# Three plain tile pairs instead of two at the start of the MLP, with the Strassen input sums split one at a time between them

## The chip, the cores and the metric

The kernel runs on one core of a Trainium2 chip. The time is device microseconds (us) for one launch. The kernel before takes 1562.86 us, the median of three runs (1561.71 to 1564.18).

## The reference, cut to what matters

Two layers (`DEPTH = 2`) over 512 tokens of width 1024. In each layer an attention mixer and a convolution mixer are merged and added to the residual `x`; then comes the MLP, which is the part that the change touches:

```python
h = rmsnorm(x, g_ffn[i])
u = dwconv(h @ w_up[i], w_ffn_conv[i])        # w_up: 1024 x 5632, width-3 conv over tokens
a, val = u[..., :D_FF], u[..., D_FF:]         # D_FF = 2816
x = x + (jax.nn.silu(a) * val) @ w_down[i]
```

After it a gated per-layer embedding is added. Everything is float32.

## The kernel before, in words

**Precision.** Each float32 operand is split into two fp32r parts, high (`h`) and low (`l`): ScalarE casts the high part (L90, L103), VectorE subtracts it from the source to get the low part (L91, L104). A product then takes three matmuls, high by high, low by high and high by low (`mm3`, L97 to L100). `load` (L81) fetches a 128x1024 weight tile of 512 KB through the SP queue into one of three `raw` buffers; `wsplit` (L86) makes `wh`, `wl` from it, five buffers each.

**Where the MLP starts.** The output projection of the mixers (L546) ends with the norm of each of the four 128-token blocks (`after_o` calls `norm`, L124 to L139): square sum on ScalarE, reciprocal root on GpSimd, scaling on VectorE (L132), four transposes into PSUM (L135) and the split into `hh`, `hl`, the transposed normalised input. It also keeps an unsplit copy of it, in four quarters `hf` (L139): `h11`, `h12`, `h21`, `h22`, by token half and by input half.

**The up projection** has 22 pairs of 128-column output tiles (`NJ = 22`, one gate tile and one value tile to a pair). It is done in two ways.

- The first `NS = 2` pairs are plain: four tiles `eo` in four PSUM banks, each 8 k-tiles x 3 matmuls. They are done in two token halves, all four tiles on tokens 0 to 255 first and then on tokens 256 to 511 (L561 to L566), so that the first half can run while the last token blocks are still in their norm. That is 4 x 2 x 24 = 192 matmuls of 256 columns.
- The other 20 pairs use a Strassen-Winograd product of 2x2 blocks (`pair`, L597 to L647): seven products of 4 k-tiles x 3 matmuls x 256 columns, 84 matmuls to a pair, in place of eight. A generator yields between the products, so that two neighbouring pairs are interleaved. I call the products of pair j in their order y(j), x(j), z(j), and then four that accumulate into x and z.

A Strassen pair needs: two weight loads (`raw` and `rawp`, L598 and L600); the splits w0 (of `r0`) and w22 (`vh`, `vl`, two buffers each); four GpSimd differences of weight blocks in place (L605 to L608); then the splits w1 and w2 of the results (`th`, `tl`). On the input side it needs differences of the quarters: four VectorE operations on `hf` (L571 to L574), the splits of three of the results into `sums` (`sh`, `sl`, L576 to L578), and the split of `h21` back into a quarter of `hh`, `hl` (L579). VectorE also adds partial products in PSUM (L628, L641, L644).

**After a tile.** `taps` (L554) reads a finished PSUM bank: one ScalarE pass (L556) and two VectorE passes (L557, L558), the three taps of the convolution. The bank is free when the last of these has read it. `gated` (L589) does SiLU, product, and split into `gth`, `gtl`. PSUM has two banks `mm`, two `sc`, one `av` and three `tp`. The tiles take `mm` and `sc` in turn; in a Strassen pair y uses `av`, x is in an `mm` bank and z in an `sc` bank.

**What sets the order.** Outside the marked regions a list scheduler orders each engine's instructions: it simulates the kernel, and among the instructions that are ready in its simulation it takes the earliest written. Each engine then runs its list in that order. In a `manual_schedule` region (L684 to L706) the order of TensorE alone is that of the program text. Before the change the text has: the plain tiles' matmuls, the four sums, the three splits of sums and the split of h21, then `taps` and `gated` of the two plain pairs (L682, L683), then the region with the loop over Strassen pairs. From the fifth pair on `downs` interleaves pieces of the down projection (`ps_tp` matmuls of 512 columns) with the pairs.

Of the kernel before, what the change touches and what calls it, by code (L numbers as in the profile page):

```python
# [19 lines left out]
P = 128  # L20
# [4 lines left out]
KD = D // P  # L25
# [10 lines left out]
FF = 2816  # L36
NJ = FF // P
EPS = 1e-6
NS = 2
NQ = 5  # L40
HS = S // 2
MAGIC = 12582912.0
# [18 lines left out]
def encoder_kernel(ctx, tc, x_in, pT, pos, inv, w_a1, w_z, w_g, w_uq, w_ukv, w_au, w_cu, w_o,  # L61
# [11 lines left out]
    hh = cp.tile([P, NT, KD, P], F32R, name="hh")  # L73
    hl = cp.tile([P, NT, KD, P], F32R, name="hl")
# [3 lines left out]
    def psum(tag="mm"):  # L78
        return ps.tile([P, S], F32, tag=tag, name="ps_" + tag, bufs={"mm": 2, "av": 1, "sc": 2, "tp": 3}[tag])

    def load(src, n=1024):  # L81
        raw = wp.tile([P, n], F32, tag="raw", name="raw", bufs=3)
        nc.sync.dma_start(raw, src)
        return raw

    def wsplit(raw, n=1024, tag="w"):  # L86
        q, bufs = {"w": (wp, 5), "t": (ffp and ffp[-1], 4), "v": (ffp and ffp[-1], 2)}[tag]
        h = q.tile([P, n], F32R, tag=tag + "h", name=tag + "h", bufs=bufs)
        lo = q.tile([P, n], F32R, tag=tag + "l", name=tag + "l", bufs=bufs)
        nc.scalar.copy(h, raw)  # L90
        nc.vector.tensor_sub(lo, raw, h.bitcast(F32))  # L91
        return h, lo

    def weight(src, n=1024):
        return wsplit(load(src, n), n)

    def mm3(o, st, mv, start, stop, more=False):  # L97
        nc.tensor.matmul(o, st[0], mv[0], start=start, stop=False, skip_group_check=more)  # L98
        nc.tensor.matmul(o, st[0], mv[1], start=False, stop=False, skip_group_check=more)  # L99
        nc.tensor.matmul(o, st[1], mv[0], start=False, stop=stop, skip_group_check=more)  # L100

    def split(hi, lo, src):
        nc.scalar.copy(hi, src)  # L103
        nc.vector.tensor_sub(lo, src, hi.bitcast(F32))  # L104
# [95 lines left out]
    def layer(l, first):  # L200
# [64 lines left out]
        def t2(nm):  # L265
            return tmp.tile([P, S], F32, tag="t2", name=nm, bufs=4)

        def ws(o, w, rhs, nk, width, off, cols=slice(0, S), ks=None):
            for k in range(nk) if ks is None else ks:
                c = slice(k * width + off, k * width + off + P)  # L270
                mm3(o, (w[0][:, c], w[1][:, c]), (rhs[0](k, cols), rhs[1](k, cols)), k == 0, k == nk - 1)

        def hsel(b):
            return lambda k, c: b[:, c.start // P:c.stop // P, k, :]

        hT = (hsel(hh), hsel(hl))
# [277 lines left out]
        def taps(i, o):  # L554
            a = t2("fa")
            nc.scalar.activation(a, o, AF.Copy, scale=wfc[:, i, 1:2])  # L556
            nc.vector.scalar_tensor_tensor(a[:, 1:], o[:, :-1], wfc[:, i, 0:1], a[:, 1:], ALU.mult, ALU.add)  # L557
            nc.vector.scalar_tensor_tensor(a[:, :-1], o[:, 1:], wfc[:, i, 2:3], a[:, :-1], ALU.mult, ALU.add)  # L558
            return a

        ew = [weight(w_up[l, i]) for i in range(2 * NS)]  # L561
        eo = [psum("sc" if i % 2 else "mm") for i in range(2 * NS)]
        for half in range(2):
            c = slice(half * 256, half * 256 + 256)
            for i in range(2 * NS):
                ws(eo[i][:, c], ew[i], hT, KD, P, 0, c)  # L566
        quarter = [(slice(None), slice(2 * r, 2 * r + 2), slice(4 * k, 4 * k + 4), slice(None))
                   for r in range(2) for k in range(2)]
        V = nc.vector
        h11, h12, h21, h22 = hf  # L570
        V.tensor_tensor(h22, h22, h21, ALU.add)  # L571
# [1 line left out]
        V.tensor_tensor(h11, h22, h11, ALU.subtract)  # L573
        V.tensor_tensor(h12, h12, h11, ALU.subtract)  # L574
        sums = []
        for src in (h22, h11, h12):  # L576
            sums.append(tuple(ff.tile([P, 2, 4, P], F32R, tag="s", name=n, bufs=6) for n in ("sh", "sl")))
            split(*sums[-1], src)  # L578
        split(hh[quarter[2]], hl[quarter[2]], h21)  # L579

        def quart(r, k0):
            return lambda k: (hh[:, 2 * r:2 * r + 2, k0 + k, :], hl[:, 2 * r:2 * r + 2, k0 + k, :])

        def summed(i):
            return lambda k: (sums[i][0][:, :, k, :], sums[i][1][:, :, k, :])
# [3 lines left out]
        def gated(j, u):  # L589
            nc.scalar.activation(u[0], u[0], AF.Silu)  # L590
            nc.vector.tensor_tensor(u[1], u[0], u[1], ALU.mult)
            if j % 2 == 0:
                q, tag = (mid, "y") if j // 4 % 2 else (ff, "gt")
                gt[j // 2] = tuple(q.tile([P, 2, S], F32R, tag=tag, name=n, bufs=4) for n in ("gth", "gtl"))
            split(gt[j // 2][0][:, j % 2, :], gt[j // 2][1][:, j % 2, :], u[1])

        def pair(j):  # L597
            r0 = load(w_up[l, 2 * j])  # L598
            r1 = ff.tile([P, 1024], F32, tag="rawp", name="rawp", bufs=2)
            nc.sync.dma_start(r1, w_up[l, 2 * j + 1])  # L600
            b11, b21, b12, b22 = r0[:, :512], r0[:, 512:], r1[:, :512], r1[:, 512:]
            w0 = wsplit(r0)
            w22 = wsplit(b22, 512, "v")
            g = nc.gpsimd
            g.tensor_tensor(b22, b12, b22, ALU.subtract)  # L605
            g.tensor_tensor(b12, b12, b11, ALU.subtract)
            g.tensor_tensor(b11, b11, b22, ALU.subtract)
            g.tensor_tensor(b21, b21, b11, ALU.subtract)  # L608
            yield

            def product(o, w, off, mv, first):
                for k in range(4):
                    c = slice(off + k * P, off + k * P + P)
                    mm3(o, (w[0][:, c], w[1][:, c]), mv(k), first and k == 0, k == 3, not first)

            def side(nm):
                return ff.tile([P, HS], F32, tag="U", name=nm, bufs=4)

            y = psum("av")[:, :HS]
            product(y, w0, 512, quart(0, 4), True)  # L620
            w1 = wsplit(r1, 1024, "t")
            yield
            m0 = psum("mm")
            x = m0[:, HS:]
            product(x, w0, 0, quart(0, 0), True)
            Y = side("Y")
            nc.scalar.copy(Y, y)
            V.tensor_tensor(m0[:, :HS], x, Y, ALU.add)  # L628
            w2 = wsplit(r0, 1024, "t")
            yield  # L630
            m1 = psum("sc")
            z = m1[:, :HS]
            product(z, w1, 0, summed(0), True)
            yield
            product(x, w2, 0, summed(1), False)
            U, Z = side("U"), side("Z")
            nc.scalar.copy(U, x)  # L637
            nc.scalar.copy(Z, z)
            yield
            product(x, w1, 512, quart(1, 0), False)  # L640
            V.tensor_tensor(m1[:, HS:], x, Z, ALU.add)  # L641
            yield
            product(z, w22, 0, summed(2), False)
            V.tensor_tensor(z, z, U, ALU.add)  # L644
            yield
            product(x, w2, 512, quart(1, 4), False)
            gated(j, [taps(2 * j, m0), taps(2 * j + 1, m1)])  # L647
# [30 lines left out]
        def advance(g, n=1):  # L678
            for _ in range(n if g else 0):
                next(g, None)  # L680

        for j in range(NS):  # L682
            gated(j, [taps(2 * j + i, eo[2 * j + i]) for i in range(2)])  # L683
        region = tc.manual_schedule(engines={mybir.EngineType.PE})  # L684
        region.__enter__()
        old, new = None, pair(NS)
        advance(new)
        for q in range(NS, NJ + 1):
            nxt = pair(q + 1) if q + 1 < NJ else None
            advance(old)  # L690
# [11 lines left out]
            old, new = new, nxt  # L702
# [45 lines left out]
    for l in range(L):  # L748
        layer(l, l == 0)
# [79 lines left out]
```

## Time and profile before

| | |
|---|---|
| median of 3 runs | 1562.86 us (1561.71 to 1564.18) |
| profiled execution | 1562.61 us, span of its trace 1560.7 us |
| mean granted TensorE clock | 0.991 |
| TensorE busy | 1515.9 us, 97% of the span |
| VectorE busy | 1039.4 us, 67% |
| ScalarE busy | 792.5 us, 51% |
| GpSimd busy | 326.2 us, 21% |

The sum of the prediction is made against the profiled execution: 1562.61 us, of which 1.9 us lie outside the span of the trace; it is 0.25 us below the median. A row of the timeline has start and duration in us, the engine, the line, the operation with output and inputs, and in brackets the idle time before it and what released it. Matmuls overlap: a 256-column matmul lasts 0.28 us by its row, but the next one starts 0.12 us after it, so prices are taken from start to start. PEld is the weight load that goes with each matmul. A row of a windows table has the stretch, its length, each engine's busy time with its count of instructions, then the granted clock, the share of the DMA engines and GB/s. A row of the waits has the total, the number of times and the longest. The MLP of layer 0 starts at 359 us of the trace and that of layer 1 at 1131 us.

### The profile page before, as it was taken

How to read it: one execution, taken by the hardware profiler on the slowest of the kernel's cores; microseconds unless marked ns; L12 is line 12 of the kernel's file. 1: busy time of each engine (PE TensorE's matmuls, PEld its weight loads, DVE VectorE, ACT ScalarE, POOL GpSimd, SP SyncE). 2: the span in 40 equal slices, each digit the busy share in tenths (PEclk: the TensorE clock that was granted, in tenths of full speed). 3: DMA queues.
4: the chain of work that ended last, by engine and by line, in shares of the span. 5: the costliest groups of instructions: out<-in, count | busy, mean ns of one | idle time of the engine just before them, and what ended most of it. 6: DMA issues, size and time to landing. Idle time of an engine off the chain costs nothing.

```text
span 1560.7 us, 22378 instructions
## 1 busy us (share of the span) xinstructions
PE 1515.9 (97%) x8776; PEld 1326.0 (85%) x8776; DVE 1039.4 (67%) x1492; ACT 792.5 (51%) x1312; POOL 326.2 (21%) x313
## 2 busy tenths in 40 slices
PE   7999999998799999999999999999979999999998
PEld 6888888888789999998888888888878999999886
DVE  7778553438787777767477776343497877777763
ACT  6678632326455455534374887232364545454452
POOL 2800000004233232310045000000043333333000
PEclk9999999999899999999999999999989999999999
DMA  6211123322333323233142102233133332333321
GB/s 208 89 58 41 55 95 94 95 82 80 98 109 95 111 93 109 96 108 108 58 135 81 41 28 82 81 107 96 55 104 101 103 114 94 105 98 97 109 75 61
DMA packets 41448, 142.32 MB, mean 91 GB/s; under 512 B 5760, under 2 KB 6272, under 8 KB 41344
## 3 DMA queue, kind: packets, MB, share of 16 engines
q1 hardware_dynamic: 41344, 140.90, 28.4%
q8 instruction: 69, 1.13, 0.3%
q14 instruction: 35, 0.29, 0.1%
HBM read 138.78 MB, written 2.10 MB: 90 GB/s over the span
## 4 chain that ended last, share of the span: by engine, by line
PE 87%; DVE 6%; DMA 2%; ACT 2%; POOL 2%; issue 1%; SPq 0%; DVEq 0%; ACTq 0%
PE ps_mm L99 13%; PE ps_mm L98 13%; PE ps_mm L100 13%; PE ps_sc L100 8%; PE ps_sc L98 7%; PE ps_sc L99 7%; PE ps_tp L99 5%; PE ps_tp L100 5%; PE ps_tp L98 5%; PE ps_av L98 2%; PE ps_av L99 2%; PE ps_av L100 2%; PE ps_tp L438 2%; DVE wl L91 1%; DVE tl L91 1%
## 5 line engine op out<-in xcount | busy, mean ns | idle before, releaser
L90 ACT CAST wh<-raw 128x1024 fp32r<-128x1024 f32 (+1 forms) x210 | 218.1, 1044 | 304.1 <-PE ps_mm L99 91.2
L91 DVE TENSOR_TENSOR wl<-raw,wh 128x1024 fp32r<-128x1024 f32 (+1 forms) x210 | 260.9, 1251 | 152.4 <-ACT wh L90 150.9
L98 PE MATMUL ps_mm<-hh,wh 128*128 128x512 f32 (+1 forms) x672 | 245.9, 366 | 12.0 <-DVE fa L558 11.4
L99 PE MATMUL ps_mm<-hl,wh 128*128 128x512 f32 (+1 forms) x672 | 241.8, 360 | 0.0
L100 PE MATMUL ps_mm<-hh,wl 128*128 128x512 f32 (+1 forms) x672 | 241.6, 360 | 0.0
L108 POOL TENSOR_SCALAR ms<-ms 128x1 f32<-128x1 f32 (+2 forms) x40 | 13.2, 329 | 759.3 <-ACT junk L127 728.5
L98 PEld LDWEIGHTS ps_mm<-hh,wh 128*128 128x128 f32 x672 | 127.6, 190 | 30.3 <-issue 11.7
L100 PEld LDWEIGHTS ps_mm<-hh,wl 128*128 128x128 f32 x672 | 127.6, 190 | 20.0
L99 PEld LDWEIGHTS ps_mm<-hl,wh 128*128 128x128 f32 x672 | 127.9, 190 | 17.4
L605 POOL TENSOR_TENSOR rawp<-rawp 128x512 f32<-128x512 f32 x40 | 55.5, 1388 | 388.5 <-DVE vl L91 388.5
L99 PE MATMUL ps_tp<-wl,gth 128*128 128x512 f32 x320 | 126.4, 395 | 0.0
L98 PE MATMUL ps_tp<-wh,gth 128*128 128x512 f32 x320 | 126.4, 395 | 0.0
L100 PE MATMUL ps_tp<-wh,gtl 128*128 128x512 f32 x320 | 126.4, 395 | 0.0
L556 ACT ACTIVATE fa<-ps_mm,wfc 128x512 f32<-128x512 f32 x44 | 30.4, 690 | 134.8 <-PE ps_mm L100 134.7
L98 PE MATMUL ps_mm<-hh,th 128*128 128x256 f32 x320 | 89.4, 280 | 2.6 <-ACT U L637 2.6
L535 DVE TENSOR_TENSOR xs<-xs,ps_tp 128x512 f32<-128x512 f32 x80 | 54.7, 684 | 53.2 <-PE ps_tp L100 52.9
L99 PE MATMUL ps_mm<-hl,th 128*128 128x256 f32 x320 | 89.1, 278 | 0.0
L100 PE MATMUL ps_mm<-hh,tl 128*128 128x256 f32 x320 | 89.0, 278 | 0.0
L100 PEld LDWEIGHTS ps_tp<-wh,gtl 128*128 128x128 f32 x320 | 60.1, 188 | 14.5
L98 PEld LDWEIGHTS ps_tp<-wh,gth 128*128 128x128 f32 x320 | 60.2, 188 | 11.4
L99 PEld LDWEIGHTS ps_tp<-wl,gth 128*128 128x128 f32 x320 | 60.1, 188 | 11.2
L557 DVE SCALAR_TENSOR_TENSOR fa<-ps_mm,wfc,fa 128x511 f32<-128x511 f32 x44 | 32.9, 748 | 49.7 <-ACT fa L556 49.7
(297 smaller groups left out, 4198.5 us busy)
## 6 DMA issues: line engine op xcount, KB each, us to landing
raw<-in_w_up_dram SPq DMA_DIRECT2D x48, 512.0 KB, 3.8
raw<-in_w_down_dram SPq DMA_DIRECT2D x44, 512.0 KB, 3.7
rawp<-in_w_up_dram SPq DMA_DIRECT2D x40, 512.0 KB, 3.6
raw<-in_w_g_dram SPq DMA_DIRECT2D x32, 512.0 KB, 3.6
raw<-in_w_z_dram SPq DMA_DIRECT2D x24, 512.0 KB, 3.7
raw<-in_w_o_dram SPq DMA_DIRECT2D x16, 512.0 KB, 3.5
raw<-in_w_pg_dram SPq DMA_DIRECT2D x16, 512.0 KB, 3.7
raw<-in_w_au_dram SPq DMA_DIRECT2D x8, 512.0 KB, 3.7
```

Of the source, the lines that this page charges most:

```text
L90: nc.scalar.copy(h, raw)
L91: nc.vector.tensor_sub(lo, raw, h.bitcast(F32))
L98: nc.tensor.matmul(o, st[0], mv[0], start=start, stop=False, skip_group_check=more)
L99: nc.tensor.matmul(o, st[0], mv[1], start=False, stop=False, skip_group_check=more)
L100: nc.tensor.matmul(o, st[1], mv[0], start=False, stop=stop, skip_group_check=more)
L108: nc.gpsimd.tensor_scalar_add(ms, ms, EPS)
L438: nc.tensor.transpose(tp[:, k * P:(k + 1) * P], pe[:, k * P:(k + 1) * P], ident)
L535: nc.vector.tensor_tensor(xs[:, t, c], xs[:, t, c], o, ALU.add)
L556: nc.scalar.activation(a, o, AF.Copy, scale=wfc[:, i, 1:2])
L557: nc.vector.scalar_tensor_tensor(a[:, 1:], o[:, :-1], wfc[:, i, 0:1], a[:, 1:], ALU.mult, ALU.add)
L605: g.tensor_tensor(b22, b12, b22, ALU.subtract)
```

## The change

`NS` becomes 3 and a new constant `NE` is 3. The first three plain tiles (`NE`) are done in token halves as before. The TensorE region begins before the taps. In it a loop over the three plain pairs makes the remaining tiles 3, 4 and 5, each in one piece of 512 tokens, does `taps` and `gated` of the pair, and then splits one of the three sums. After the second plain pair (`j == 1`), pair 3, now the first Strassen pair, is created and its first step is written: its two loads, w0, w22 and its four GpSimd differences. The split of `h21` comes after the loop. The four additions of L571 to L574 stay where they are, ahead of the loop. Strassen pairs are 3 to 21, 19 to a layer in place of 20; the main loop starts at q = 3.

```diff
-NS = 2
+NS = 3
+NE = 3
...
-        ew = [weight(w_up[l, i]) for i in range(2 * NS)]
-        eo = [psum("sc" if i % 2 else "mm") for i in range(2 * NS)]
+        ew = [weight(w_up[l, i]) for i in range(NE)]
+        eo = [psum("sc" if i % 2 else "mm") for i in range(NE)]
         for half in range(2):
             c = slice(half * 256, half * 256 + 256)
-            for i in range(2 * NS):
+            for i in range(NE):
                 ws(eo[i][:, c], ew[i], hT, KD, P, 0, c)
-        quarter = [(slice(None), slice(2 * r, 2 * r + 2), slice(4 * k, 4 * k + 4), slice(None))
-                   for r in range(2) for k in range(2)]
...
         sums = []
-        for src in (h22, h11, h12):
+
+        def sumsplit(src):
             sums.append(tuple(ff.tile([P, 2, 4, P], F32R, tag="s", name=n, bufs=6) for n in ("sh", "sl")))
             split(*sums[-1], src)
-        split(hh[quarter[2]], hl[quarter[2]], h21)
...
-        for j in range(NS):
-            gated(j, [taps(2 * j + i, eo[2 * j + i]) for i in range(2)])
         region = tc.manual_schedule(engines={mybir.EngineType.PE})
         region.__enter__()
-        old, new = None, pair(NS)
-        advance(new)
+        for j in range(NS):
+            u = []
+            for i in (2 * j, 2 * j + 1):
+                if i >= NE:
+                    eo.append(psum("sc" if i % 2 else "mm"))
+                    ws(eo[i], weight(w_up[l, i]), hT, KD, P, 0)
+                u.append(taps(i, eo[i]))
+            gated(j, u)
+            sumsplit((h22, h11, h12)[j])
+            if j == 1:
+                old, new = None, pair(NS)
+                advance(new)
+        q = (slice(None), slice(2, 4), slice(0, 4), slice(None))
+        split(hh[q], hl[q], h21)
         for q in range(NS, NJ + 1):
```

## Prediction

> **What bounds the kernel now.** I read the page first, then TensorE's waits, then the timeline of the MLP's start engine by engine, then windows.
>
> ```profile
> span 1560.7 us, 22378 instructions
> PE 1515.9 (97%) x8776; PEld 1326.0 (85%) x8776; DVE 1039.4 (67%) x1492; ACT 792.5 (51%) x1312; POOL 326.2 (21%) x313
> ```
>
> TensorE is the bound over the whole span; a change can win only what TensorE waits for, or what it does slowly. Who makes it wait:
>
> ```profile
> PE ps_mm L98 <- DVE fa L558: 11.4, 2, 5.7
> PE ps_sc L98 <- DVE fa L558: 7.2, 2, 3.6
> PE ps_sc L100 <- DVE tl L91: 5.9, 4, 1.9
> PE ps_mm L98 <- ACT U L637: 2.6, 3, 1.6
> ```
>
> The two largest are each met twice, once a layer: a Strassen product waits for the last tap (L558) of a plain tile, which holds its PSUM bank. All four lie at the start of the MLP. TensorE's timeline there, layer 0:
>
> ```profile
> 358.97 0.29 PE L98 MATMUL ps_mm<-hh,wh 128*128 128x256 f32 x1
> ...
> 367.81 0.60 PE L135 MATMUL ps_tp<-ident,ht 128*128 128x128 f32 x4
> ...
> 383.27 0.28 PE L98 MATMUL ps_av<-hh,wh 128*128 128x256 f32 x1
> ...
> 384.56 0.28 PE L100 MATMUL ps_av<-hh,wl 128*128 128x256 f32 x1
> 390.52 0.55 PE L98 MATMUL ps_mm<-hh,wh 128*128 128x256 f32 x1 [5.68 <-DVE fa L558]
> ...
> 393.00 0.41 PE L100 MATMUL ps_mm<-hh,wl 128*128 128x256 f32 x1
> 397.04 0.55 PE L98 MATMUL ps_sc<-sh,th 128*128 128x256 f32 x1 [3.62 <-DVE fa L558]
> ...
> 404.43 0.39 PE L98 MATMUL ps_mm<-hh,th 128*128 128x256 f32 x1 [1.62 <-ACT U L637]
> ...
> 418.26 0.39 PE L98 MATMUL ps_sc<-sh,th 128*128 128x256 f32 x1 [0.74 <-ACT th L90]
> ...
> 420.70 0.58 PE L100 MATMUL ps_sc<-sh,tl 128*128 128x256 f32 x1 [1.93 <-DVE tl L91]
> ...
> 433.68 0.39 PE L100 MATMUL ps_sc<-sh,tl 128*128 128x256 f32 x1 [1.41 <-DVE tl L91]
> ```
>
> The plain tiles run from 358.97 without a wait. The first product of pair 2 follows at 383.27; then x(2) waits, z(2) waits, and smaller waits follow to 433.68. The clock falls too:
>
> ```profile
> 390.00:391.00 1.00, 0.48 (x2) 0.51 (x3) 1.00 (x3) 0.55 (x1) 0.84 (x1) 0.50 0.47 188
> ...
> 421.00:422.00 1.00, 1.00 (x6) 1.00 (x6) 1.00 (x3) 0.62 (x1) 0.00 (x0) 0.50 0.49 66
> ```
>
> After each long stall the granted clock is 0.50 for a while: the 11 steps from 390.52 to 393.00 take 2.48 us, and the same 11 from 383.27 to 384.56 take 1.29. A dozen matmuls at the low clock cost 1.2 us extra.
>
> The cause is VectorE's list:
>
> ```profile
> 370.41 1.23 DVE L571 TENSOR_TENSOR hf<-hf 128x1024 f32<-128x1024 f32 x1 [0.65 <-ACT hf L139]
> ...
> 378.51 2.32 DVE L574 TENSOR_TENSOR hf<-hf 128x1024 f32<-128x1024 f32 x1
> ...
> 382.99 0.74 DVE L557 SCALAR_TENSOR_TENSOR fa<-ps_mm,wfc,fa 128x511 f32<-128x511 f32 x1
> ...
> 389.64 0.74 DVE L558 SCALAR_TENSOR_TENSOR fa<-ps_mm,wfc,fa 128x511 f32<-128x511 f32 x1
> ...
> 402.58 0.68 DVE L104 TENSOR_TENSOR gtl<-fa,gth 128x512 fp32r<-128x512 f32 x1
> ```
>
> None of the later rows has an idle time in brackets: VectorE is full from 370.4 to 403, and tile 0's second tap is run only at 389.64, behind sums and weight splits. So the stage has both a full engine and a bad order on it. The size of the loss:
>
> ```profile
> 1131.13:1155.43 24.30, 24.30 (x209) 24.29 (x208) 20.71 (x20) 15.86 (x23) 10.27 (x7) 1.00 0.32 112
> 1155.43:1206.26 50.83, 38.03 (x279) 36.75 (x278) 44.24 (x52) 26.39 (x39) 19.47 (x12) 0.87 0.30 93
> 358.97:383.27 24.30, 24.30 (x210) 24.30 (x208) 20.71 (x20) 15.86 (x23) 10.27 (x7) 1.00 0.37 112
> 383.27:436.42 53.15, 38.15 (x278) 36.89 (x277) 44.22 (x52) 26.27 (x39) 19.49 (x12) 0.87 0.29 88
> ```
>
> The windows end where the first matmul of a down piece starts. The second window of each layer holds 23 products of 12 matmuls, 276. At full speed:
>
> ```profile
> 369.19 0.28 PE L98 MATMUL ps_sc<-hh,wh 128*128 128x256 f32 x1
> ...
> 371.89 0.28 PE L100 MATMUL ps_sc<-hh,wl 128*128 128x256 f32 x1
> ...
> 436.42 0.39 PE L98 MATMUL ps_tp<-wh,gth 128*128 128x512 f32 x1
> ...
> 438.99 0.39 PE L100 MATMUL ps_tp<-wh,gtl 128*128 128x512 f32 x1
> ```
>
> 23 steps of a 256-column matmul take 2.70 us, 0.1175 each; 11 of a 512-column one take 2.57, 0.2335 each. 276 x 0.1175 = 32.4 us. The loss is 53.15 - 32.4 = 20.7 us in layer 0 and 50.83 - 32.4 = 18.4 in layer 1, **39.1 us in all**. That is the most that can be won.
>
> **The change part by part.**
>
> *More matmul work.* Before: 192 x 0.1175 = 22.56 plus a Strassen pair of 84 x 0.1175 = 9.87, 32.43 us a layer. After: three tiles in halves, 144 x 0.1175 = 16.92, and three whole, 72 x 0.2335 = 16.81, 33.73. **+1.3 us a layer, +2.6**. It is on the path, with certainty.
>
> *Shorter cover for the last norm.* Token block 3's transposes end at about 368.4 (row at 367.81), and its splits just after:
>
> ```profile
> 368.39 1.37 DVE L104 TENSOR_TENSOR hl<-ps_tp,hh 128x512 fp32r<-128x512 f32 x2 [2.42 <-ACT hh L103]
> ```
>
> The first half of three tiles is 72 x 0.1175 = 8.5 us plus the 16 transposes (24.30 - 22.56 = 1.7 us), so TensorE would want block 3 at 358.97 + 10.2 = 369.2; the first of the two splits ends near 369.1, the second at 369.76 and is wanted four k-tiles (1.4 us) later. Before, one more tile (2.8 us) covered this. I take 0.5 us a layer, between 0 and 2.8.
>
> *The two big waits.* The halves end at 358.97 + 16.92 + 1.7 = 377.6; tile 3 runs to 383.2, tile 4 to 388.8, tile 5 to 394.4; then y(3), x(3), z(3) at 394.4, 395.8, 397.2. Tile 4 reuses the bank of tile 0 and tile 5 that of tile 1; x(3) needs taps of tile 2, z(3) those of tile 3. The taps of tiles 0 and 1 are now written ahead of all splits of sums and of all weight splits but the first tiles'. VectorE has, from 370.4: four sums at 1.23 (4.9 us), then taps of two tiles at 2 x 0.74 each (3.0). They end near 379 by the price of the rows, and tile 4 wants the first at 383.2. So both waits, 5.68 and 3.62, and the 2.4 us of low clock behind them go, unless the order says otherwise (a rival).
>
> *What is late next.* VectorE's work up to z(4), at 394.4 + 7 x 1.41 = 404.3: four sums 4.9; twelve tap passes 8.9; nine subtractions of 1024 columns (wl of tiles 4, 5 and of w0 of two pairs; tl of both first parts and the first pair's second; two sums) and h21's,
>
> ```profile
> L91 DVE TENSOR_TENSOR wl<-raw,wh 128x1024 fp32r<-128x1024 f32 x31 | 37.2, 1222 | 10.6 <-ACT wh L90 10.6
> ```
>
> 10 x 1.22 = 12.2; eight passes of 512 or 256 columns at no more than 0.68 (two vl, two products, two gtl, two adds), some 5.0. That is 31 us in 33.9 (370.4 to 404.3). To it comes GpSimd's toll:
>
> ```profile
> 379.71 2.28 POOL L605 TENSOR_TENSOR rawp<-rawp 128x512 f32<-128x512 f32 x1
> ...
> L91 DVE TENSOR_TENSOR wl<-raw,wh 128x1024 fp32r<-128x1024 f32 x3 | 5.8, 1935 | 0.0
> ```
>
> L574 takes 2.32 us in GpSimd's company where L571 took 1.23, and three wl between 370.4 and 403 took 1.94 each against 1.22 later: 1.1 + 3 x 0.72 = 3.3 us, and I take 4 for two pairs. So 35 in 33.9: VectorE is about just in time, and z(4) waits by 0 to 5 us. I take 2.4, and 1.0 more for a dozen matmuls at the low clock behind it.
>
> The Trainium skill ("SBUF — State Buffer", section "Who interferes with whom") says that a VectorE instruction with two SBUF inputs and a GpSimd one that reads SBUF exclude each other, the later waiting for the whole of the other. By this rule the change doesn't remove the toll, it moves it under the plain tiles; the 2.32 us agrees.
>
> *The vh chain.* vh, vl have two buffers, so a pair's w22 waits for the product of two pairs earlier:
>
> ```profile
> 410.95 0.61 ACT L90 CAST vh<-rawp 128x512 fp32r<-128x512 f32 x1
> ...
> 413.31 1.30 POOL L605 TENSOR_TENSOR rawp<-rawp 128x512 f32<-128x512 f32 x1 [22.47 <-DVE vl L91]
> ...
> 418.69 1.96 DVE L91 TENSOR_TENSOR tl<-rawp,th 128x1024 fp32r<-128x1024 f32 x1
> ```
>
> From vh to the end of tl lie 9.7 us, with five products (7.1 us) between in TensorE's order. Before, pairs 4 and 5 pay it with no down piece as cover (0.74 + 1.93, and 1.41). After, pair 4 is only the second Strassen pair and finds a free buffer; pair 5 still pays: 1.6 a layer, between 0.7 and 2.7. The wait for U (1.62 in layer 0, 2.6 in both) comes from ScalarE's queue behind a down weight that is still loading; nothing in the change removes it; 1.0 a layer.
>
> *Queues passed.* Pair 3's two loads go ahead of tiles 4 and 5 in SP's text and its GpSimd work ahead of their matmuls.
>
> ```profile
> raw<-in_w_up_dram SPq DMA_DIRECT2D x48, 512.0 KB, 3.8
> ```
>
> At 3.8 us a load, with three buffers that come free as the first tiles' splits end (before 370), tiles 4 and 5 have their weights ahead of 383 and 389; what hides this is tile 3's 5.6 us. Behind a late load would wait ScalarE's casts, then taps. I put it at nothing, up to 2 us.
>
> **The sum.** What stays a layer: 0.5 + 2.4 + 1.0 + 1.6 + 1.0 = 6.5 us. 1562.61 - 39.1 + 2.6 + 2 x 6.5 = **1539 us**. The median stands 0.25 above the profiled run, which is nothing here. The terms' ends, 2 to 11 a layer, give 1530 to 1548.
>
> A clock rule: the trace grants 0.50 at 421 after 0.74 and 1.93 us of idle with two matmuls between. The Trainium skill ("TensorE: Matmul & The Clock Gate", "HAM oscillation — how this bites in real kernels") asks for an idle gap of some 3.4 us before the clock drops. By the page the 1.0 us of low clock would be 0 and the sum 1537; the row speaks for keeping it.
>
> **The rivals.**
> 1. *VectorE's backlog only shifts* (0.15). Its work up to the fourth pair grows by two splits, two tiles' taps and a gate, 2.4 + 3.0 + 1.4 = 6.8 us, TensorE's cover by tiles 4 and 5, 11.2; if throughput and not order made the 12 us of the two waits and their clock, 12 - (11.2 - 6.8) = 7.6 stay beside the 4 to 6 elsewhere, 13 a layer: 1562.6 - 39.1 + 2.6 + 26 = 1552. For it: no idle VectorE for 33 us. Against: much of what ran there wasn't due yet.
> 2. *Tile 4 takes over the wait: slower* (0.08). If the scheduler leaves tile 0's second tap where it is (end 390.4), tile 4, due at 383.2, waits 7.2 us in place of x(2)'s 5.8, and all else behind it stays: 1.4 + 1.3 a layer, 1568. It decides for any tap end after about 388. Against: the splits that stood ahead of it are now written after it.
> 3. *Nearly all of it goes* (0.14): the later waits were echoes of the first stall. 1 to 2 us stay a layer: 1562.6 - 39.1 + 2.6 + 3 = 1529.
> 4. *It doesn't matter* (0.03): the waits reappear behind tile 5 in equal size, within 3 us of 1562.
>
> **How the numbers follow.** The forecast has 0.60. A measurement can tell about 0.2%, 3 us, from no change. Faster: 0.60 + 0.15 + 0.14 = 0.89; same 0.03; slower 0.08. The range goes from rival 3's end to just past rival 1: 1528 to 1555.
>
> **What would show it.** In the profile after: waits for L558 near zero; TensorE unbroken from 359 to about 397, with 72 matmuls of 512 columns more a layer (whole plain tiles); clock 1.00 there; tile 0's second tap before 383; one wait at a Strassen z for tl of 1 to 3 us in place of two; U's still there. A gap ahead of the 512-column plain tiles would be rival 2, gaps of 5 us after 395 rival 1, and a gap near 369 would mean that three tiles don't cover the norm.

## The result and the profile after

The changed kernel takes **1547.28 us** (median of four runs, 1546.78 to 1548.68). The kernel before, run beside it, takes 1562.78 (1561.71 to 1564.18). The ratio is 0.9902 with a 95% interval of [0.9885, 0.9919]: faster by 15.5 us, about two thirds of the 23.5 that were forecast. The time lies in the predicted range, 8 us above the predicted value. The profiled execution of after is the slowest of its four, 1548.68 us.

The page, its span and its first engine row:

```profile
span 1546.9 us, 22111 instructions
PE 1514.3 (98%) x8656; PEld 1318.1 (85%) x8656; DVE 1029.3 (67%) x1482; ACT 788.4 (51%) x1302; POOL 309.3 (20%) x305
```

TensorE's busy time hardly moves (1515.9 before) while the span falls by 13.8 us. So most of the gain is waiting that went away. What is left of the four waits that the prediction showed:

```profile
PE ps_mm L99 <- DVE fa L559: 14.5, 2, 7.2
...
PE ps_sc L101 <- DVE tl L92: 1.1, 2, 0.6
```

The columns are the total, the number of times and the longest. Line numbers up to the taps are one higher than before: L559 is the last tap, which was L558. The two large waits of before (5.7 and 3.6 a layer) have become one of 7.2 a layer, the waits at `tl` fell from four to two, and the wait for U is gone. TensorE's timeline at the start of layer 0's MLP, from the end of tile 3:

```profile
383.24 0.39 PE L101 MATMUL ps_sc<-hh,wl 128*128 128x512 f32 x1
390.87 0.76 PE L99 MATMUL ps_mm<-hh,wh 128*128 128x512 f32 x1 [7.24 <-DVE fa L559]
...
396.55 0.41 PE L100 MATMUL ps_mm<-hl,wh 128*128 128x512 f32 x1
...
404.75 0.28 PE L99 MATMUL ps_av<-hh,wh 128*128 128x256 f32 x1
...
425.78 0.39 PE L101 MATMUL ps_sc<-sh,tl 128*128 128x256 f32 x1 [0.56 <-DVE tl L92]
...
428.51 0.39 PE L99 MATMUL ps_tp<-wh,gth 128*128 128x512 f32 x1
```

The halves and tile 3 run without a gap; the last matmul of tile 3 starts at 383.24, within 0.3 us of what was worked out. Then tile 4 (390.87) waits for tile 0's second tap, whose bank it takes: this is the gap that the prediction named as the sign of its second rival. Behind it 13 matmuls run at the low clock, 5.68 us (390.87 to 396.55) where 13 x 0.2335 = 3.04 were due. From there to the first down piece at 428.51 only 0.56 us is waited for; y(3), x(3) and z(3) (404.75 to 407.56) follow tile 5 without a gap.

The loss of the stage, reckoned as in the prediction: from the end of tile 3 (383.24 + 0.23) to the first down piece, in each layer.

```profile
383.47:428.51 45.04, 37.24 (x241) 33.94 (x241) 39.36 (x47) 24.88 (x35) 11.20 (x8) 0.89 0.30 96
1147.50:1192.75 45.25, 37.44 (x243) 34.11 (x241) 39.61 (x47) 25.06 (x35) 11.32 (x8) 0.89 0.30 96
```

It holds tiles 4 and 5, 48 matmuls at 0.2335, and 16 products, 192 at 0.1175: 33.8 us at full speed. The loss is 11.3 us in layer 0 and 11.5 in layer 1, where before it was 20.7 and 18.4. Put into the prediction's sum: 1562.6 - 39.1 + 2.6 + 22.8 = 1548.9, and the profiled run shows 1548.7. So nothing outside these windows moved and the added matmul work was right; the residual was taken at 13 and is 22.8.

VectorE's list up to the tap that tile 4 waits for, every row:

```profile
370.54 1.23 DVE L571 TENSOR_TENSOR hf<-hf 128x1024 f32<-128x1024 f32 x1 [0.65 <-ACT hf L140]
371.80 1.22 DVE L572 TENSOR_TENSOR hf<-hf 128x1024 f32<-128x1024 f32 x1
372.94 0.69 DVE L92 TENSOR_TENSOR vl<-rawp,vh 128x512 fp32r<-128x512 f32 x1
373.54 1.22 DVE L573 TENSOR_TENSOR hf<-hf 128x1024 f32<-128x1024 f32 x1
374.68 2.32 DVE L105 TENSOR_TENSOR sl<-hf,sh 128x1024 fp32r<-128x1024 f32 x1
376.92 1.79 DVE L92 TENSOR_TENSOR vl<-rawp,vh 128x512 fp32r<-128x512 f32 x1
378.63 2.32 DVE L92 TENSOR_TENSOR wl<-raw,wh 128x1024 fp32r<-128x1024 f32 x1
380.87 2.31 DVE L574 TENSOR_TENSOR hf<-hf 128x1024 f32<-128x1024 f32 x1
383.11 0.74 DVE L558 SCALAR_TENSOR_TENSOR fa<-ps_mm,wfc,fa 128x511 f32<-128x511 f32 x1
383.77 1.64 DVE L92 TENSOR_TENSOR wl<-raw,wh 128x1024 fp32r<-128x1024 f32 x1
385.33 2.28 DVE L105 TENSOR_TENSOR sl<-hf,sh 128x1024 fp32r<-128x1024 f32 x1
387.53 0.74 DVE L558 SCALAR_TENSOR_TENSOR fa<-ps_sc,wfc,fa 128x511 f32<-128x511 f32 x1
388.19 1.21 DVE L92 TENSOR_TENSOR tl<-rawp,th 128x1024 fp32r<-128x1024 f32 x1
389.32 0.73 DVE L558 SCALAR_TENSOR_TENSOR fa<-ps_mm,wfc,fa 128x511 f32<-128x511 f32 x1
389.99 0.73 DVE L559 SCALAR_TENSOR_TENSOR fa<-ps_mm,wfc,fa 128x511 f32<-128x511 f32 x1
```

Tile 0's second tap runs at 389.99. Before the change it ran at 389.64, though it is now written ahead of two splits of sums and of other pairs' weight splits. Seven rows that the prediction left behind the taps stand ahead of this one: two `vl`, two `sl`, two `wl` and a `tl`. From start to start they take, in the order of this sentence, 0.60 + 1.71 + 2.24 + 2.20 + 2.24 + 1.56 + 1.13 = 11.7 us: about what lies between the 379 at which the prediction let the taps end and the 390.7 of the trace. Six of the rows are longer than the same operations elsewhere (four of 2.3 and one of 1.64 against 1.22, one of 1.79 against 0.69). GpSimd runs beside them, and is itself slowed, from 1.30 for one alone to between 1.63 and 2.28:

```profile
376.00 2.16 POOL L606 TENSOR_TENSOR rawp<-rawp,raw 128x512 f32<-128x512 f32 x1
378.24 1.63 POOL L607 TENSOR_TENSOR raw<-raw,rawp 128x512 f32<-128x512 f32 x1
379.83 2.28 POOL L605 TENSOR_TENSOR rawp<-rawp 128x512 f32<-128x512 f32 x1
```

### The profile page after: what moved, and what is told of

Read it like the earlier page. It is cut to its first block, busy times and chain, and to the rows that moved or that the text cites. A ratio compares the mean times of both kernels' runs of the same rounds, so it can differ in the third digit from the quotient of the medians.

```text
span 1546.9 us, 22111 instructions
## 1 busy us (share of the span) xinstructions
PE 1514.3 (98%) x8656; PEld 1318.1 (85%) x8656; DVE 1029.3 (67%) x1482; ACT 788.4 (51%) x1302; POOL 309.3 (20%) x305
## 4 chain that ended last, share of the span: by engine, by line
PE 92%; DVE 3%; POOL 2%; issue 1%; ACT 1%; DMA 1%; SPq 0%; DVEq 0%; ACTq 0%
PE ps_mm L99 14%; PE ps_mm L100 14%; PE ps_mm L101 14%; PE ps_sc L99 8%; PE ps_sc L101 8%; PE ps_sc L100 8%; PE ps_tp L100 5%; PE ps_tp L101 5%; PE ps_tp L99 5%; PE ps_av L99 2%; PE ps_av L100 2%; PE ps_av L101 2%; PE ps_tp L439 2%; PE ps_tp L136 1%; PE ps_av L451 1%
## 5 line engine op out<-in xcount | busy, mean ns | idle before, releaser
L99 PE MATMUL ps_mm<-hh,wh 128*128 128x512 f32 (+1 forms) x680 | 251.1, 369 | 15.0 <-DVE fa L559 14.5
L100 PE MATMUL ps_mm<-hl,wh 128*128 128x512 f32 (+1 forms) x680 | 247.0, 363 | 0.0
L101 PE MATMUL ps_mm<-hh,wl 128*128 128x512 f32 (+1 forms) x680 | 246.5, 363 | 0.0
L99 PE MATMUL ps_mm<-hh,th 128*128 128x256 f32 x304 | 84.6, 278 | 0.0
L100 PE MATMUL ps_mm<-hl,th 128*128 128x256 f32 x304 | 84.6, 278 | 0.0
L101 PE MATMUL ps_mm<-hh,tl 128*128 128x256 f32 x304 | 84.6, 278 | 0.0
L99 PEld LDWEIGHTS ps_tp<-wh,gth 128*128 128x128 f32 x320 | 60.2, 188 | 11.3
L100 PEld LDWEIGHTS ps_tp<-wl,gth 128*128 128x128 f32 x320 | 60.1, 188 | 11.2
L558 DVE SCALAR_TENSOR_TENSOR fa<-ps_mm,wfc,fa 128x511 f32<-128x511 f32 x44 | 32.9, 747 | 50.1 <-ACT fa L557 50.1
```

## The experiments

Four theories of why tile 4 waits were to be told apart:

- the **bank**: only the reuse of tile 0's PSUM bank brings VectorE's lateness to TensorE, and without it the 10 us of wait and low clock would go;
- the **order**: VectorE's list has enough time and wrong priorities, so a better order removes the wait;
- **throughput**: VectorE has more work than time between 370 and about 410, so wherever the wait is removed, one of much the same size comes a little later;
- the **toll**: a part of that work is the time that GpSimd's company adds to VectorE's rows, 5.9 us up to tile 0's second tap (five rows 1.1 longer, one 0.43) and 0.7 behind it, so some 6.6 us a layer.

A further question was which part of the edit made the gain. In the table the waits are those of TensorE in layer 0 of the profile, from 383 us on, in us.

| kernel | median | ratio to before, 95% | waits, in their order |
|---|---|---|---|
| after | 1547.28 | 0.9902 [0.9885, 0.9919] | 7.24, 0.56 |
| two plain pairs, new order | 1563.30 | 0.9999 [0.9990, 1.0008] | as before |
| three pairs, sums' splits first | 1547.59 | 0.9900 [0.9883, 0.9916] | 7.2, 0.6 |
| other banks for tiles 4, 5 | 1546.64 | 0.9891 [0.9876, 0.9906] | 6.92, 0.55 |
| idle matmuls in the wait | 1555.58 | 0.9947 [0.9930, 0.9963] | 0.70, 5.10, 0.55 |
| VectorE's order by hand | 1549.43 | 0.9912 [0.9897, 0.9927] | 7.74, 1.31 |
| four plain pairs | 1546.03 | 0.9888 [0.9873, 0.9902] | 6.17 |
| four, other banks | 1546.54 | 0.9891 [0.9876, 0.9905] | 6.34 |
| small GpSimd differences | 1535.13 | 0.9817 [0.9803, 0.9832] | 0.79, 0.66, 1.48, 0.57 |
| differences on VectorE | 1543.24 | 0.9869 [0.9852, 0.9885] | 1.99, 2.94, 0.98 |
| the same, four pairs, other banks | 1541.52 | 0.9858 [0.9843, 0.9872] | 3.62 |
| the same, three pairs, other banks | 1537.41 | 0.9831 [0.9816, 0.9846] | 0.33, 2.12, 0.59, 0.90 |

### Which part of the edit gains

Two plain pairs, all four tiles in halves, and the rest of the change kept: the region from before the taps, the sums' splits written between the pairs.

```diff
-NS = 3
-NE = 3
+NS = 2
+NE = 4
...
             sumsplit((h22, h11, h12)[j])
-            if j == 1:
-                old, new = None, pair(NS)
-                advance(new)
+        sumsplit(h12)
+        old, new = None, pair(NS)
+        advance(new)
```

> Two plain pairs as in the kernel before, all four tiles in token halves, and only the order of the text changed: the sums are split one by one behind each gated pair, the first Strassen pair begins behind them, and the TensorE region begins ahead of the taps. If the order of the splits is what wins, 1547 to 1552 us. If the third plain pair is what wins, no change: 1560 to 1564 us.

The ratio is 0.9999 [0.9990, 1.0008], and the four waits that the prediction showed are those of before within 0.2 us (11.4, 7.2, 6.1 and 2.5 over both layers). The new place of the splits in the text does nothing by itself.

The other half, three plain pairs with the splits ahead of the taps, was first made with h21's split ahead of them too.

```diff
+        for src in (h22, h11, h12):
+            sumsplit(src)
+        q = (slice(None), slice(2, 4), slice(0, 4), slice(None))
+        split(hh[q], hl[q], h21)
         region = tc.manual_schedule(engines={mybir.EngineType.PE})
...
             gated(j, u)
-            sumsplit((h22, h11, h12)[j])
...
-        q = (slice(None), slice(2, 4), slice(0, 4), slice(None))
-        split(hh[q], hl[q], h21)
```

> Three plain pairs, three tiles in halves, as in the changed kernel, but all three sums and h21 are split in the text ahead of the taps, as in the kernel before, and pair 3 begins where it does in the changed kernel. If the third plain pair is what wins, 1546 to 1550 us; if the order of the splits is, 1557 us or more.

It takes 1553.60 us (0.9936 [0.9922, 0.9951]), but says nothing of the sums: tiles 3 to 5 here read the differenced quarter, and TensorE waits 9.54 us in layer 0 for h21's own split, within tile 3. So it was made again, with that split left behind the loop:

```diff
+        for src in (h22, h11, h12):
+            sumsplit(src)
         region = tc.manual_schedule(engines={mybir.EngineType.PE})
...
             gated(j, u)
-            sumsplit((h22, h11, h12)[j])
```

> The changed kernel with one thing put back: the three sums are split in the text ahead of the taps of all plain pairs (h21's split stays behind the loop, since tiles 3 to 5 still read that quarter). Three pairs and the rest as changed. If splitting them one by one matters, 1552 us or more, as the wait at tile 4 grows by the 2.4 us of the two later sums in each layer; if the scheduler gives VectorE the same list either way, 1546 to 1549.

```profile
389.93 0.73 DVE L559 SCALAR_TENSOR_TENSOR fa<-ps_mm,wfc,fa 128x511 f32<-128x511 f32 x1
```

1547.59 us, as after, with the same 7.2 us wait. Tile 0's second tap is at 389.93, where after has it at 389.99. With all three splits written ahead of the taps, or with two of them behind, VectorE gets nearly the same list. The whole gain comes with the third plain pair; the splitting one by one has none of it. What came with that pair in the same edit, three tiles in halves in place of four and pair 3 begun early, was not tried apart.

### Bank, order or throughput

Tiles 4 and 5 into `tp` banks, so that no tile waits for the taps of tiles 0 and 1:

```diff
-                    eo.append(psum("sc" if i % 2 else "mm"))
+                    eo.append(psum("tp" if i > 3 else "sc"))
```

> Plain tiles 4 and 5 get a third and fourth kind of PSUM bank (tp, idle here) in place of those of tiles 0 and 1, so tile 4 no longer waits for tile 0's second tap; nothing else is edited. Theory A, the bank: the 7.2 us wait and the 2.5 us of low clock behind it go in each layer, 19.5 us in all, 1528 us. Theory B, VectorE's throughput: its list is as long as before, so the wait comes back at the first Strassen products (banks of tiles 0 to 2, the split of h21), 4 to 8 us a layer, 1538 to 1545 us.

TensorE's wait, and the VectorE addition that ends it:

```profile
405.97 0.58 PE L99 MATMUL ps_mm<-sh,th 128*128 128x256 f32 x1 [6.92 <-DVE ps_mm L628]
```

```profile
405.50 0.42 DVE L628 TENSOR_TENSOR ps_mm<-ps_mm,Y 128x256 f32<-128x256 f32 x1
```

The gap at 383 is gone, TensorE runs through to 399, and then it waits 6.92 us for an addition of 0.42 us that stands in VectorE's list behind taps, splits and a gate. The time is 1546.64, 1.6 us above the range that the expectation gave to throughput. The bank theory falls as the cause: the bank decided where VectorE's lateness was paid, not whether.

Then the wait was filled: 28 idle matmuls of 512 columns ahead of tile 4, so that the clock stays up.

```diff
-                    ws(eo[i], weight(w_up[l, i]), hT, KD, P, 0)
+                    wi = weight(w_up[l, i])
+                    if i == 4:
+                        idle = psum("tp")
+                        for k in range(28):
+                            nc.tensor.matmul(idle, ew[2][0][:, :P], hh[:, :, 0, :], start=k == 0, stop=k == 27)
+                    ws(eo[i], wi, hT, KD, P, 0)
```

> 28 idle matmuls of 512 columns (28 x 0.2335 = 6.5 us) into an unused PSUM bank stand on TensorE ahead of tile 4, inside the 7.2 us wait; their result is read by nobody. If the low clock behind the wait costs 13 matmuls x 0.19 us = 2.5 us a layer, the time falls by 5 us to about 1542. If the clock costs nothing, or VectorE is what is late next, the time stays within 1.5 us of 1547. If the fillers push tile 4 back, it rises.

```profile
390.87 0.47 PE L99 MATMUL ps_mm<-hh,wh 128*128 128x512 f32 x1 [0.70 <-DVE fa L559]
...
411.74 0.58 PE L99 MATMUL ps_mm<-sh,th 128*128 128x256 f32 x1 [5.10 <-DVE ps_mm L628]
```

Tile 4 starts at the very time of after, 390.87, and without the low clock; and the kernel is 8 us slower than after, a rise that the expectation gave only for a tile 4 pushed back. TensorE, 2.6 us earlier through tile 4, now waits 5.10 us for the addition of L628, with a low clock of its own behind it. The addition itself runs later, at 411.26 against 408.58 in after. VectorE's list has changed a little, and just before the addition VectorE idles for a ScalarE cast, which waits 4.78 us for the load of a down weight:

```profile
409.45 1.23 DVE L92 TENSOR_TENSOR wl<-raw,wh 128x1024 fp32r<-128x1024 f32 x1 [2.13 <-ACT wh L91]
```

In after, in its place:

```profile
408.58 0.42 DVE L628 TENSOR_TENSOR ps_mm<-ps_mm,Y 128x256 f32<-128x256 f32 x1
```

So of the 5.10 us, 2.4 are TensorE's being earlier: in after, the slow stretch behind the wait was time that VectorE used. The other 2.7 are VectorE's being later, 2.13 of them idle, and don't measure its throughput.

Third, VectorE's order in this stretch was written out by hand: four sums, then both taps of tile 0 and tile 1, and only then the rest.

```diff
+        region = tc.manual_schedule(engines={mybir.EngineType.PE, mybir.EngineType.DVE})
+        region.__enter__()
+        u = [taps(0, eo[0]), taps(1, eo[1])]
+        w4 = weight(w_up[l, 4])
+        gated(0, u)
+        u = [taps(2, eo[2])]
+        old, new = None, pair(NS)
+        advance(new)
+        sumsplit(h22)
...
+        region.__exit__(None, None, None)
```

> The changed kernel with VectorE's order written out for the plain part: the four sums, taps of tiles 0 and 1, the weights of tile 4, the first gate, taps of tile 2, then pair 3's first weights, and each sum's split after that; behind it the scheduler's list as before. Tile 4's wait goes. Order theory: what was ahead of the taps wasn't due, nothing of size takes its place, 2 x 9 us less, 1530 us. Throughput theory: VectorE is full to 411 us, and the wait comes back at pair 3's products, 1542 to 1547.

```profile
375.92 0.75 DVE L559 SCALAR_TENSOR_TENSOR fa<-ps_mm,wfc,fa 128x511 f32<-128x511 f32 x1
```

```profile
406.55 0.55 PE L99 MATMUL ps_mm<-sh,th 128*128 128x256 f32 x1 [7.74 <-DVE ps_mm L629]
```

Tile 0's taps are done at 376.7, 14 us earlier than in after, tile 4 doesn't wait, and the wait of 7.74 us comes back at the same kind of addition (L629 here). The time of 1549.43 is 2.4 us above the end of the throughput range. The order theory falls for this order at least; no other order was written by hand. Three kernels that take the wait away from tile 4 by three means get 6.92, 5.10 and 7.74 us at the first Strassen pair's addition. That speaks for throughput, but it doesn't rule out the order: in each list this small addition stands behind splits and taps. In the kernel with the order by hand, seven splits that are written behind the hand-ordered part (a `vl`, two `wl`, three `tl` and the `hl`) run among its rows from 387 on, ahead of that addition.

Would more TensorE work ahead give VectorE its time? A fourth plain pair, first in the banks `mm` and `sc`:

```diff
-NS = 3
+NS = 4
...
-            sumsplit((h22, h11, h12)[j])
+            if j < 3:
+                sumsplit((h22, h11, h12)[j])
...
-            if old and q % 4 == 0:
+            if q % 4 == 0:
```

> Four plain pairs, three tiles in halves and five whole; 18 Strassen pairs a layer. It costs TensorE 1.3 us more a layer. Throughput theory: two tiles more are 11.2 us of cover against 6.8 us of VectorE work, but the wait at tile 4 stands ahead of that cover and stays at 7.2 us; nothing is left to win behind it, so 1550 us. If lateness behind tile 4 still costs something, 1544 or less.

and then with `tp` banks for tiles 4 to 7 as well (the change of the first experiment on top):

> Four plain pairs, and tiles 4 to 7 in tp banks, so that neither waits for the taps of tile 0. Throughput theory: the 6.2 us wait and its low clock (1.7 us) before tile 4 move behind 22 us of plain tiles, whose VectorE work is shorter by 4 to 5 us than their matmuls; 3 to 5 us of wait are left at the first Strassen pair: 1538 to 1542 us. If the lateness can't be covered by plain tiles, 1546 as with four pairs alone.

They take 1546.03 and 1546.54, within 1.3 us of after. The first still waits at tile 4 (6.17 us), and its time lies between the two that were expected. In the second, TensorE runs through to 400; there are three `tp` banks, so tile 7 takes that of tile 4, and VectorE reaches tile 4's last tap only at 405.73:

```profile
405.73 0.74 DVE L559 SCALAR_TENSOR_TENSOR fa<-ps_tp,wfc,fa 128x511 f32<-128x511 f32 x1
```

```profile
406.61 0.77 PE L99 MATMUL ps_tp<-hh,wh 128*128 128x512 f32 x1 [6.34 <-DVE fa L559]
```

The throughput range of the second, 1538 to 1542, missed this: 11 us more of cover don't help while a bank still ties the cover to the list that is late.

### The toll

GpSimd's four differences of the first two Strassen pairs, on 16 of 512 columns (the other columns stay undifferenced):

```diff
             g = nc.gpsimd
+            if j < NS + 2:
+                b11, b21, b12, b22 = (b[:, :16] for b in (b11, b21, b12, b22))
```

> GpSimd's four weight differences of the first two Strassen pairs are cut from 512 to 16 columns; the rest of these weight blocks stays undifferenced, and nothing else is left out. In the changed kernel's trace the VectorE rows beside GpSimd's add up to 6.6 us over their price alone. Toll theory: VectorE's list runs some 6 us sooner, the wait at tile 4 falls from 7.2 to about 1 us without low clock, and the time falls by 2 x 8 us to about 1531. Order theory, in which the toll is a side matter: the wait stays at 5 us or more, 1542 or more.

```profile
374.77 1.24 DVE L105 TENSOR_TENSOR sl<-hf,sh 128x1024 fp32r<-128x1024 f32 x1
375.94 0.70 DVE L92 TENSOR_TENSOR vl<-rawp,vh 128x512 fp32r<-128x512 f32 x1
...
383.63 0.73 DVE L559 SCALAR_TENSOR_TENSOR fa<-ps_mm,wfc,fa 128x511 f32<-128x511 f32 x1
```

```profile
384.51 0.47 PE L99 MATMUL ps_mm<-hh,wh 128*128 128x512 f32 x1 [0.79 <-DVE fa L559]
```

The rows that took 2.32 and 1.79 us take 1.24 and 0.70, tile 0's second tap is 6.4 us earlier (5.8 by shorter rows, 0.7 since tile 2's first tap now stands behind it), tile 4's wait falls from 7.24 to 0.79, and the clock stays at 1.00. The time is 1535.13, 12 us under after: 6 a layer, near the size of the toll, and 4 above the 1531 that was expected. The toll is shown. The Trainium skill ("SBUF — State Buffer", section "Who interferes with whom") states that a VectorE instruction with two SBUF inputs and a GpSimd instruction that reads SBUF share a read port. It fits these rows: the taps, which have one input in PSUM, hold their 0.74 us in GpSimd's company.

That kernel leaves work out. One that leaves nothing out moves the same differences to VectorE:

```diff
-            g = nc.gpsimd
+            g = V if j < NS + 2 else nc.gpsimd
```

> The changed kernel, with the four weight differences of the first two Strassen pairs on VectorE in place of GpSimd. VectorE has eight operations of 512 columns more, 8 x 0.68 = 5.4 us a layer. Toll theory: the 6.6 us that GpSimd's company cost it go, and the wait is about 1 us shorter a layer: 1543 to 1547 us. If the toll is small, VectorE is later by 5 us a layer, 1555 or more.

```profile
L607 DVE TENSOR_TENSOR raw<-raw,rawp 128x512 f32<-128x512 f32 x2 | 1.4, 686 | 0.0
```

Each costs 0.68 us there (0.60 from start to start), eight of them 4.8 us, against the 6.6 that they cost VectorE from GpSimd's side. 1543.24 us, 4 less than after. The engine that was late gets through its list earlier by taking on more work: the first pair's addition runs at 403.89, where after has it at 408.58.

Then both edits together, with four plain pairs and with three:

> Four plain pairs, tiles 4 to 7 in tp banks, and the first two Strassen pairs' weight differences on VectorE. Throughput theory: VectorE's lateness is 1 us smaller than with GpSimd, and the scheduler now counts this work when it makes VectorE's list, so that the small additions due early stand nearer to their time: 1534 to 1540 us.

> Three plain pairs, tiles 4 and 5 in tp banks, and the first two Strassen pairs' weight differences on VectorE. Throughput theory: the 6.9 us wait for the first addition of Y, met with tp banks alone, shrinks, since the scheduler's plan now holds all of VectorE's work, but what is due later becomes late: 1536 to 1543 us. If the list's order is a side matter and only the sum of work counts, 1543 to 1546.

Four take 1541.52, a little above what was expected: tile 7 waits 3.62 us for tile 4's bank, with a low clock behind it. Three take **1537.41 us**, the least of the kernels that do the whole work, 1.7% under before and 10 us under after. TensorE's largest waits in this kernel, and the window of tiles 4 and 5:

```profile
416.70 0.36 PE L99 MATMUL ps_mm<-hh,wh 128*128 128x256 f32 x1 [2.12 <-DVE fa L559]
...
418.95 0.36 PE L99 MATMUL ps_sc<-sh,th 128*128 128x256 f32 x1 [0.59 <-DVE fa L559]
...
420.32 0.39 PE L101 MATMUL ps_sc<-sh,tl 128*128 128x256 f32 x1 [0.90 <-DVE tl L92]
```

```profile
383.47:404.00 20.53, 20.39 (x126) 17.98 (x125) 20.53 (x27) 12.03 (x17) 0.00 (x0) 1.00 0.25 86
```

TensorE is busy for 20.39 of the 20.53 us in which after stood for 7.4. The backlog is paid at 415 to 420 instead, 3.6 us in pieces, and none of them brings the clock down.

Here the order counts. VectorE has the same work in this kernel as in the one of 1543.24 us, but the first pair's addition runs 6.1 us earlier. It stands ahead of three `tl`, two `gtl` and two taps, 5.9 us of rows, that come before it in the other list. There it runs at 403.89, here at

```profile
397.77 0.42 DVE L628 TENSOR_TENSOR ps_mm<-ps_mm,Y 128x256 f32<-128x256 f32 x1
```

With other banks alone TensorE waited 6.92 us for this addition. Less work by 1.8 us (6.6 - 4.8) would leave some 5, an estimate; here no wait is left at it. The expectation had 1543 to 1546 for the case that only the sum of work counts, and 1537.41 lies in its other range. So the order counts beside the toll and the sum of the work. Why the scheduler comes to this list is only argued, and this order without the move of the differences wasn't tried.

## Why the prediction was right or wrong

- **More matmul work, +2.6 us**: right. With it the sum closes to 0.2 us of the profiled run.
- **Norm cover, 0.5 a layer**: nothing. No row between 359 and 383 has an idle time.
- **The two big waits and their low clock go**: this is the step that failed, and it failed in one sentence, that the taps of tiles 0 and 1 "end near 379 by the price of the rows". That took the order of the text for the order of VectorE's list. The list up to tile 0's second tap hardly changed, and the runs with the splits moved in the text (1563.30, 1547.59) show that this order moves nothing here. Why the scheduler comes to that list, by the times of its own simulation as the section on the kernel has it, is only argued. And the order by hand shows that early taps alone bring nothing: the wait comes back behind tile 5.
- **GpSimd's toll, 4 us**: 6.6 by the rows, and shown to be the cause of most of the wait by leaving it out. The trace of before already had 7.0: the term counted L574 and the `wl`, and left out an `sl` of 1.65 us (at 383.65) and these:

```profile
374.56 2.32 DVE L104 TENSOR_TENSOR sl<-hf,sh 128x1024 fp32r<-128x1024 f32 x1
376.80 1.79 DVE L91 TENSOR_TENSOR vl<-rawp,vh 128x512 fp32r<-128x512 f32 x1
...
385.23 2.28 DVE L91 TENSOR_TENSOR tl<-rawp,th 128x1024 fp32r<-128x1024 f32 x1
```

- **VectorE's list up to z(4), 35 us with the toll**: VectorE is full from 370.5 to 410.8, 40 us. Up to there its list holds 15 splits of 1024 columns where the sum has 10. How much of the loss these five make was not tried apart.
- **z(4) waits 2.4, U 1.0, low clock 1.0**: z(4) and U don't wait at all, the low clock costs 2.6. The likely cause of the first is that TensorE stood for 7.4 us at tile 4 and went slowly for 5.7, and VectorE caught up meanwhile. The idle matmuls bear this out for 2.4 us; why U's wait went was not looked into.
- **The vh chain**: right in place, once a layer and only for the pair that the prediction named, but 0.56 us and not 1.6.
- **Rival 2** had the wait right to a tenth (7.2 us, tap end after 388) and the consequence wrong: it kept everything behind it in place, and nearly everything went. So its 1568 was far off. **Rival 1**, that the backlog only shifts, describes the stage best; its 13 us a layer stand against 11.3 measured, its 1552 against 1547.
- **The gain itself**: in place of a Strassen pair, 9.9 us of TensorE that need sums and differences, stands a plain pair of 11.2 us that needs neither. The loss falls from 39.1 to 22.8 us, by 16.3, and the work grows by 2.6: 13.7 us, where the two spans differ by 13.8.

The predicted 6.5 us of residual a layer were 2.4 + 1.0 + 1.6 + 1.0 + 0.5; the measured 11.3 are 7.4 + 2.6 + 0.6 and some 0.7 in slow first matmuls behind waits. The number came near by luck: small waits that were forecast and didn't come made up for half of the large one that did.

## What to carry to other kernels

Where an engine has no idle row for 30 us, find what inflates its rows before reordering it or giving its consumer another bank: alone, both only moved the wait here. Then ask of each fix where in the late list the next instruction stands that another engine needs. Compare the list of the late engine row by row before and after the edit, since what is written earlier need not run earlier under a list scheduler. Work moved to a neighbour engine isn't free if the neighbour's company slows the engine that was to be relieved.

## What the runs showed of the hardware

In this stretch, eight subtractions of 128x512 cost VectorE more when GpSimd does them (6.6 us in longer rows) than when VectorE does them itself (8 x 0.60 = 4.8). GpSimd takes 1.30 us for one alone and up to 2.28 beside VectorE; VectorE takes 0.68.

The clock fell after idle times of different lengths. In the kernel with the differences on VectorE a single wait of 2.94 us was enough:

```profile
404.00:405.00 1.00, 0.64 (x4) 0.64 (x5) 1.00 (x3) 0.00 (x0) 0.00 (x0) 0.92 0.52 201
405.00:406.00 1.00, 1.00 (x7) 1.00 (x6) 1.00 (x1) 0.63 (x1) 0.00 (x0) 0.50 0.64 258
```

It didn't fall after 2.12, 0.59 and 0.90 us within 5 us (the kernel of 1537.41 us), nor after 1.48 (small GpSimd differences). The Trainium skill ("TensorE: Matmul & The Clock Gate", section "HAM oscillation — how this bites in real kernels") asks for an idle gap of more than some 3.4 us; the 2.94 us wait speaks against taking that as a bound. How long matmuls then run at the low clock varied as well: 5.7 us behind the 7.24 us wait, about 3.4 behind the 2.94.
